# A two-layer encoder on one core: idle TensorE products and a pinned order at the opening, earlier q swaps and later value products in the last layer

## The chip, the core and the metric

The kernel runs on one core of a Trainium2 chip. A core has five engines that work side by side, each in the order of its own instruction stream: TensorE (PE in the profile, with its weight loads shown as PEld), VectorE (DVE), ScalarE (ACT), GpSimd (POOL) and SyncE (SP), which here only issues transfers (DMAs). They wait for each other through semaphores. The metric is the time of one execution in microseconds; less is better.

## The reference

Two layers over 272 tokens (16 learned ones and 256 given) of width 2048. Cut to what matters:

```python
for i in range(DEPTH):                                  # DEPTH = 2
    h = _rmsnorm(h_stream, norm_mix[i])
    proj = h @ w_in[i]                                  # q | k | v | f | ga | gf
    q = _rope_2d(_rmsnorm(q, q_norm[i]), cos_r, sin_r, cos_c, sin_c)     # 8 heads of 128
    k = _rope_2d(_rmsnorm(k, k_norm[i]), cos_r, sin_r, cos_c, sin_c)     # 2 heads
    s = einsum('bqkgd,bskd->bkgqs', q, k) / sqrt(128);  p = softmax(s);  attn = einsum(p, v)
    a_br = attn @ w_attn_br[i]
    s_br = fft2(f over tokens and group channels).real @ w_four[i]
    merged = sigmoid(ga) * a_br + sigmoid(gf) * s_br
    h_stream = h_stream + merged @ w_out[i]
    h2 = _rmsnorm(h_stream, norm_ffn[i])
    u_gate = _dwconv3_centred((h2 @ w_up[i])[..., :D_FF], w_conv[i], b_conv[i])
    h_stream = h_stream + (silu(u_gate) * (h2 @ w_up[i])[..., D_FF:]) @ w_down[i]
return h_stream[:, N_META:]
```

All is float32.

## The kernel before

**Tiling.** Activations lie channels by tokens: 16 tiles of 128 channels x 272 tokens. To keep float32 accuracy each operand is split into a high part and the remainder (`xH`, `xL`; `wh`, `wl`), and each product is made of three: high x high, high x low, low x high. Weights stream in chunks of 512 KB (four blocks of 128 rows x 256 columns). One chunk is loaded into one of four `raw` buffers by SP (`load_raw`, L264), ACT casts it into `wh` (L306), DVE subtracts that into `wl` (L308), and TensorE multiplies it: 24 products of 272 columns.

**Order.** A planner orders each engine's instructions by the order in which they are traced and by when it thinks that their inputs are there. `tc.keep_in_program_order` pins an instruction behind the one traced before it on its engine. `tc.manual_schedule` keeps the traced order of the engines that it names for a whole block.

**Groups and shadow work.** `group` runs the products of one block of weight columns. After every six products it calls `step`, which advances one of the generators in `shadow` (work that shares the engines with the groups: norms, rotary embedding, Fourier transform, attention). A `yield n` asks for n steps of pause; `push(gen, n)` starts a generator after n steps. `next_split` calls `advance`, which loads ahead by the four buffers, and `pump`, which traces the casts and subtractions.

**The opening.** Four columns of the layer's Fourier projection come first (`first_groups`, L420 on), two at a time, while XT and the first weights still arrive. Chunk 0 comes in pieces (L486 to L488) and so do the first tiles of XT; `norm_split` (L520) makes `xH` on ACT and `xL` on DVE, and `norm_sum` (L527) squares a tile on ACT and adds it up on DVE for the norm. The load of chunk 1 (L491) waits for a tiny GpSimd copy into its buffer (L490), which itself reads chunk 0.

**The last layer's mixing part.** The order of groups is k, v, q0, q1, f4 (the folded Fourier columns, `folded_f`), q2, q3, then the gates ga and gf. For each q group `head_evac` (L927) leaves the scaled heads in `qp` and their squares in `qps`; `q_stage` (L1037) swaps 32-row blocks with four transfers on SP (`swap`, L946), sums the squares through TensorE transposes, and rotates (`rope`, L952). `kstats` (L975) does the same for k. `attend` runs `attention` once for each of the two k heads: per item scores (L1085), softmax (`normalise`), transposes of the weights into `PH` and `PL` (`transposed`, L1116), and per head the value products (`values`, L1138), whose operands are `PH` and `PL` of the whole head. The items follow each other step by step in the loop at L1148.

Of the kernel before, what the change touches and what calls it, by code (L numbers as in the profile page):

```python
# [10 lines left out]
F32 = mybir.dt.float32  # L11
# [150 lines left out]
def encoder_kernel(ctx, tc, xT, params, consts, bmat, cfold, csign, w_fl, w_f64c, w_in, w_abr, w_four, w_f64, w_out, w_up, w_down, w_vn, w_dn, w_dt, out):  # L162
# [79 lines left out]
            chunks.append(ch)  # L242
    st = {"raw": 0, "fetch": 0, "next": 0, "grp": 0, "stage": None}
    raws, splits = {}, {}
    RAW, LOOK = 4, 2

    def extra(i):
# [51 lines left out]
    def split_w(i, a, b, parts="hl"):  # L299
        if i not in splits:  # L300
            splits[i] = tuple(weight_rows(wp.tile([P, CW * CS], F32R, tag=t, name=f"{t}{i}"), i in streamed) for t in ("wh", "wl"))
        h, lo = splits[i]
        st["wl"] = lo
        r = raws[i]
        if "h" in parts:
            nc.scalar.copy(h[:, a:b], r[:, a:b])  # L306
        if "l" in parts:
            nc.vector.tensor_tensor(lo[:, a:b], r[:, a:b], h[:, a:b].bitcast(F32), op=ALU.subtract)  # L308
            if b == CW:
                del raws[i]  # L310

# [165 lines left out]
    o64m = per.tile([P, P], F32, name="o64m")  # L477
    small = ctx.enter_context(tc.tile_pool(name="small", bufs=4))

    nc.gpsimd.dma_start(remE[:, 0, 0:1], chunks[1][0][:, 0, 0:1])  # L480
    nc.gpsimd.memset(mhalf, -0.5)
    nc.scalar.dma_start(prm[:, 0:P_BG], params[:, 0:P_BG])
    nc.scalar.activation(warm, mhalf[:, 0:1], AF.Copy)
    r0 = wp.tile([P, CW, MG * P], F32, tag="raw", name="raw0", bufs=RAW)
# [2 lines left out]
        nc.sync.dma_start(XT[:, c0:c1, :], xT[:, c0:c1, :])  # L487
        nc.sync.dma_start(r0[:, c0:c1], chunks[0][0][:, c0:c1])  # L488
    raws[1] = wp.tile([P, CW, MG * P], F32, tag="raw", name="raw1", bufs=RAW)
    nc.gpsimd.tensor_copy(raws[1][:, 0, 0:1], r0[:, 0, 0:1])  # L490
    tc.keep_in_program_order(nc.sync.dma_start(raws[1], chunks[1][0]))  # L491
    tc.keep_in_program_order(nc.sync.dma_start(XT[:, 4:8, :], xT[:, 4:8, :]))
    load_raw(2)
    load_raw(3)
    st["raw"] = 4
    tc.keep_in_program_order(nc.sync.dma_start(XT[:, 8:12, :], xT[:, 8:12, :]))
    nc.gpsimd.memset(ones, 1.0)
    nc.gpsimd.memset(V3.bitcast(F32), 0.0)
    nc.gpsimd.memset(o64.bitcast(F32), 0.0)
    nc.gpsimd.memset(o64m, 0.0)  # L500
    nc.gpsimd.memset(remE, 0.0)
# [18 lines left out]
    def norm_split(m, goff):  # L520
        gc = prm[:, goff + m:goff + m + 1]
        xH, xL = (xHLs[goff // KT % DEPTH][:, r] for r in range(2))
        nc.scalar.activation(xH[:, m, :], XT[:, m, :], AF.Copy, scale=gc)
        nc.vector.scalar_tensor_tensor(xL[:, m, :], XT[:, m, :], gc, xH[:, m, :].bitcast(F32),
                                       op0=ALU.mult, op1=ALU.subtract)

    def norm_sum(m):  # L527
        sq = small.tile([P, T], F32, tag="sq", name="sq", bufs=2)
        nc.scalar.activation(sq, XT[:, m, :], AF.Square)
        if m == 0:  # L530
            nc.vector.tensor_copy(acc, sq)
        else:
            nc.vector.tensor_tensor(acc, acc, sq, op=ALU.add)
# [100 lines left out]
    for l in range(DEPTH):  # L634
# [7 lines left out]
        with tc.tile_pool(name=f"mix{l}", bufs=1) as mp:  # L642
# [105 lines left out]
            if l == 0:  # L748
                def sums(pss):
                    for m in range(KT):  # L750
                        norm_sum(m)
                        yield 4 if m % 4 == 3 else 1
                    yield from norm_stats(hold, 4)
                    yield 3
                    for i in range(2):
                        f_evac(i, pss[i])
                        yield 2
                    hold["evac"] = True

                pss = []  # L760
                push(sums(pss), 4)
                first_groups(pss)
                for dst, src in ((cst[:, 0:C_MASK], consts[:, 0:C_MASK]), (cst[:, C_CC:], consts[:, C_CC:]), (prm[:, P_BG:], params[:, P_BG:])):
                    tc.keep_in_program_order(nc.sync.dma_start(dst, src))
                bt = rt("bt")
                bt = bt[:, :, :TH]
                tc.keep_in_program_order(nc.sync.dma_start(bt, bmat.rearrange("p (a b) -> p a b", a=2)))
                with tc.manual_schedule(engines={mybir.EngineType.PE, mybir.EngineType.DVE}):
                    ps = group((l, "f", 2), xr(0), T, "aux")
                until(hold, "evac")  # L770
                f_evac(2, ps)
                nc.scalar.copy(BH, bt)
                tc.keep_in_program_order(nc.vector.tensor_tensor(BL, bt, BH.bitcast(F32), op=ALU.subtract))
                nc.gpsimd.memset(br3[96:P].bitcast(F32), 0.0)
                for a in (0, 32):
                    nc.scalar.copy(br3[a:a + 32], brem[a:a + 32])
                tc.keep_in_program_order(nc.vector.tensor_tensor(br3[64:96], brem[32:64], br3[32:64].bitcast(F32), op=ALU.subtract))
                tc.keep_in_program_order(nc.vector.tensor_scalar(bgh, prm[:, P_BG:P_BG + DEPTH * 2 * KT], 0.5, None, op0=ALU.mult))
                f_evac(3, group((l, "f", 3), xr(0), T))
            else:  # L780
                push(norm_stats(hold), 8)
                nc.gpsimd.memset(remE, 0.0)
                nc.gpsimd.memset(remO, 0.0)
                w64c = rw("w64c").rearrange("p a b -> p (a b)")[:, :KT * NG].rearrange("p (k r) -> p k r", k=KT)
                nc.sync.dma_start(w64c, w_f64c)
                w64s = mp.tile([P, 2, 2 * TH], F32R, tag="r", name="w64s", bufs=7)
                w64s = w64s.rearrange("p a b -> p (a b)")[:, :KT * 2 * NG].rearrange("p (k r) -> p k r", k=KT)
                nc.scalar.copy(w64s[:, :, 0:NG], w64c)
                nc.vector.tensor_tensor(w64s[:, :, NG:], w64c, w64s[:, :, 0:NG].bitcast(F32), op=ALU.subtract)
# [185 lines left out]
            def kstats():  # L975
# [4 lines left out]
                nc.vector.tensor_scalar(kss, kss, 1.0 / HD, EPS, op0=ALU.mult, op1=ALU.add)  # L980
                rk = small.tile([P, 2, 3], F32, tag="rk", name="rk")
                pow_half(rk.rearrange("p a b -> p (a b)"), kss.rearrange("p a b -> p (a b)"))
                yield 6
                for kv in range(NKV):
                    dk = ut("dk")
                    for i, (a, b) in enumerate(BLK):
# [8 lines left out]
                yield from rope(kp, qs, kH, kL)  # L995
                hold["keys"] = True

            push(kstats(), 4)
            if last:
                slots = fold_setup()  # L1000
                push(fold_ahead(slots), 2)
# [32 lines left out]
            for pn in pns:  # L1034
                nc.gpsimd.memset(pn[:, 0:P], 0.0)

            def q_stage(i, qp, qsq):  # L1037
                kv, j = i // 2, i % 2
                sl = slice(2 * j, 2 * j + 2)
                if j == 0:  # L1040
                    qvs.append(small.tile([P, 9], F32, tag="qv", name="qv"))
                    qsms.append(small.tile([P, 2, 4, NM], F32, tag="sqm", name="sqm", bufs=2))
                qv, qsm = qvs[kv], qsms[kv]
                qs = swap(qp)
                yield 3
                nc.vector.tensor_copy(qsm[:, :, 2 * j:2 * j + 2, :], qsq[:, :, 0:NM].unsqueeze(1).to_broadcast([P, 2, 2, NM]))
                d4 = qv[:, 4 * j:4 * j + 4]
                sums_t(d4, [qsq[:, m, a:b] for m in range(MG) for a, b in BLK[1:]])
                d4 = d4.rearrange("p (m i) -> p m i", m=2)
                nc.vector.tensor_tensor(d4, d4, bc2(tok2[:, 1:3]), op=ALU.mult)  # L1050
                if j:
                    yield 1
                    sums_t(qv[:, 8:9], [qsm.rearrange("p r h t -> p (r h t)")])
                    nc.vector.tensor_tensor(qv[:, 8:9], qv[:, 8:9], tok2[:, 0:1], op=ALU.mult)
                    nc.vector.tensor_scalar(qv, qv, 1.0 / HD, EPS, op0=ALU.mult, op1=ALU.add)
                    rq = small.tile([P, 9], F32, tag="rq", name="rq")
                    pow_half(rq, qv)
                yield 6 - j
                yield from rope(qp, qs, qH[kv][:, sl, :], qL[kv][:, sl, :])
                if j:  # L1060
                    rqs.append(rq)
                    if kv == 0:
                        push(attend(), 5)
# [7 lines left out]
                    yield from attention(kv, rqs[kv])  # L1071

            def attention(kv, rq):
                nc.vector.tensor_scalar(rq, rq, 1.0 / math.sqrt(HD), None, op0=ALU.mult)
                qm = mp.tile([P, 2, 2, 4, NM], F32R, tag="qm", name="qm")
                for j, src in enumerate((qH, qL)):
                    nc.scalar.copy(qm[:, j], src[kv][:, :, 0:NM].bitcast(F32).unsqueeze(1).to_broadcast([P, 2, 4, NM]))
# [68 lines left out]
                    nc.vector.tensor_tensor(qL[kv][:, h, lo:T], po[:, :W], qH[kv][:, h, lo:T].bitcast(F32), op=ALU.subtract)  # L1146

                items = [None] + [(h, i) for h in range(4) for i in range(2)]  # L1148
                prev, ready, due = None, [], []
                for item in items + ["end", "end"]:  # L1150
                    cur = None
                    if item != "end":
                        pe, sm = scores(item)
                    yield 2
                    if item != "end":
                        cur = (item, normalise(pe, sm))
                    yield 1
                    if prev is not None:
# [1 line left out]
                        if prev[0] is not None and prev[0][1] == 1:  # L1160
                            due.append(prev[0][0])
                        yield 1
                    if ready:
                        values(ready.pop(0))
                    if prev is not None:
                        yield 1
                    ready, due = ready + due, []
                    prev = cur
                while ready:
                    values(ready.pop(0))  # L1170
                    yield 1

            qH, qL = [], []
            for i in range(4):
# [17 lines left out]
                if last and i == 1:  # L1192
# [5 lines left out]
                            folded_f(slots, E)  # L1198
                    o1_tiles()
                    push(folded_chan(E), 1)  # L1200
                push(q_stage(i, *qq), 1)


            def gate(kind, i):
# [401 lines left out]
```

## Time and profile before

| what | time |
|---|---|
| median of 3 runs | 2517.09 us (2516.09 to 2518.9) |
| profiled execution, its own time | 2520.21 us |
| its span, first to last instruction | 2518.4 us |
| mean granted TensorE clock over the span | 0.998 |
| TensorE busy | 2503.5 us |

The span is what the views of the trace show; the execution's own time is 1.8 us longer. In lists of waits the columns are: who waited, for whom, then the total in us, how often, and the longest. In a timeline: start, length in us, engine, line, operation, what it writes and reads, and in brackets the engine's idle time before it with what ended that. Merged rows have a count (x4).

### The profile page before, as it was taken

The numbers are of one execution on the slowest core, as the hardware profiler recorded it, in microseconds if no ns is written. First come the engines' busy times: TensorE is split into PE (matmuls) and PEld (weight loads), VectorE is DVE, ScalarE is ACT, GpSimd is POOL, SyncE is SP. The second block draws the span as 40 slices with busy tenths as digits, with TensorE's granted clock in tenths as the row PEclk, the third lists the DMA queues.
The fourth block names the chain that finished last, engine by engine and source line by source line (L and its number), as shares of the span: only waits on it lengthen the run. The fifth ranks groups of instructions, "written<-read, shape, count | busy, mean of one in ns | idle before, by whom it ended". The sixth has DMA issues, their size and how long they took to land. (4 is left out here: it accounts for less than half of the span.)

```text
span 2518.4 us, 47932 instructions
## 1 busy us (share of the span) xinstructions
PE 2503.5 (99%) x18848; PEld 2423.2 (96%) x18848; DVE 1988.6 (79%) x3159; ACT 1339.9 (53%) x1913; POOL 203.9 (8%) x394
## 2 busy tenths in 40 slices
PE   9999999999999999999999999999999999999999
PEld 9999999999999999999999999999988899999987
DVE  7687866778878677888768877666879787898898
ACT  6455534454444334444445555444676665666665
POOL 0000000012212222222200000000000000000000
PEclk9999999999999999999999999999999999999999
DMA  7444557879999999999975547888888887788887
GB/s 248 166 156 163 188 198 245 261 267 378 396 335 378 407 384 374 397 381 379 400 268 177 193 141 224 272 262 261 259 260 293 298 289 241 260 282 290 280 301 272
DMA packets 194802, 706.85 MB, mean 281 GB/s; under 512 B 22144, under 2 KB 27392, under 8 KB 194320
## 3 DMA queue, kind: packets, MB, share of 16 engines
q1 hardware_dynamic: 146768, 517.09, 58.4%
q0 software_dynamic: 46368, 184.57, 21.1%
q8 instruction: 147, 2.41, 0.4%
q10 hardware_dynamic: 1440, 2.13, 0.2%
q14 instruction: 79, 0.65, 0.1%
HBM read 623.32 MB, written 111.15 MB: 292 GB/s over the span
## 5 line engine op out<-in xcount | busy, mean ns | idle before, releaser
L306 ACT CAST wh<-raw 128x1024 fp32r<-128x1024 f32 (+1 forms) x961 | 998.6, 1044 | 888.9 <-PE ps_ug L378 190.2
L308 DVE TENSOR_TENSOR wl<-raw,wh 128x1024 fp32r<-128x1024 f32 (+1 forms) x961 | 1159.2, 1218 | 391.0 <-ACT wh L306 378.1
L377 PE MATMUL ps_ug<-xHL,wh 128*128 128x272 f32 (+1 forms) x1408 | 401.1, 285 | 0.0
L379 PE MATMUL ps_ug<-xHL,wl 128*128 128x272 f32 (+1 forms) x1408 | 399.4, 285 | 0.0
L378 PE MATMUL ps_ug<-xHL,wh 128*128 128x272 f32 (+1 forms) x1408 | 399.1, 284 | 0.0
L377 PEld LDWEIGHTS ps_ug<-xHL,wh 128*128 128x128 f32 x1408 | 265.4, 188 | 3.2
L378 PEld LDWEIGHTS ps_ug<-xHL,wh 128*128 128x128 f32 x1408 | 265.0, 188 | 3.2
L379 PEld LDWEIGHTS ps_ug<-xHL,wl 128*128 128x128 f32 x1408 | 264.7, 188 | 1.1 <-DVE wl L308 0.4
L1446 PE MATMUL ps_p<-wh,opnd 128*128 128x512 f32 x816 | 222.3, 393 | 0.0
L379 PE MATMUL ps_uv<-xHL,wl 128*128 128x272 f32 x704 | 202.2, 287 | 0.0
L379 PE MATMUL ps_d<-gHL,wl 128*128 128x272 f32 x704 | 202.1, 287 | 0.0
L377 PE MATMUL ps_uv<-xHL,wh 128*128 128x272 f32 x704 | 201.7, 286 | 0.0
L377 PE MATMUL ps_d<-gHL,wh 128*128 128x272 f32 x704 | 201.5, 286 | 0.0
L378 PE MATMUL ps_uv<-xHL,wh 128*128 128x272 f32 x704 | 201.0, 285 | 0.0
L378 PE MATMUL ps_d<-gHL,wh 128*128 128x272 f32 x704 | 201.0, 285 | 0.0
L1446 PEld LDWEIGHTS ps_p<-wh,opnd 128*128 128x128 f32 x816 | 148.5, 188 | 28.5 <-ACT wh L306 0.2
L377 PE MATMUL ps_ga<-xHL,wh 128*128 128x272 f32 (+1 forms) x512 | 148.6, 290 | 0.0
L377 PE MATMUL ps_gf<-xHL,wh 128*128 128x272 f32 (+1 forms) x512 | 147.0, 287 | 0.0
L540 DVE TENSOR_TENSOR wi<-wi,wi 128x512 f32<-128x512 f32 x224 | 146.9, 685 | 0.0
L378 PE MATMUL ps_ga<-xHL,wh 128*128 128x272 f32 (+1 forms) x512 | 146.2, 286 | 0.0
L379 PE MATMUL ps_ga<-xHL,wl 128*128 128x272 f32 (+1 forms) x512 | 146.2, 286 | 0.0
L379 PE MATMUL ps_o<-mH,wl 128*128 128x272 f32 (+1 forms) x512 | 146.0, 285 | 0.0
(380 smaller groups left out, 5974.0 us busy)
## 6 DMA issues: line engine op xcount, KB each, us to landing
raw<-in_w_up SPq DMA_DIRECT2D x288, 512.0 KB, 6.4
raw<-in_w_in SPq DMA_DIRECT2D x191, 512.0 KB, 4.2
raw<-in_w_down SPq DMA_DIRECT2D x88, 512.0 KB, 7.3
wi<-in_w_dn POOLq DMA_DIRECT2D x80, 512.0 KB, 9.3
ft<-wi POOLq DMA_DIRECT2D x80, 512.0 KB, 7.7
raw<-ft SPq DMA_DIRECT2D x80, 512.0 KB, 4.7
raw<-in_w_out SPq DMA_DIRECT2D x64, 512.0 KB, 4.2
raw<-fv SPq DMA_DIRECT2D x64, 512.0 KB, 4.8
```

Source lines behind the costliest of these rows:

```text
L306: nc.scalar.copy(h[:, a:b], r[:, a:b])
L308: nc.vector.tensor_tensor(lo[:, a:b], r[:, a:b], h[:, a:b].bitcast(F32), op=ALU.subtract)
L377: nc.tensor.matmul(o, h[:, c, sl], a, start=kt == 0, stop=False)
L378: nc.tensor.matmul(o, h[:, c, sl], b, start=False, stop=False)
L379: nc.tensor.matmul(o, lo[:, c, sl], a, start=False, stop=kt == nk - 1)
L540: tt = lambda *v, **kw: tc.keep_in_program_order(nc.vector.tensor_tensor(*v, **kw))
L1446: nc.tensor.matmul(ps[h], x, w[:, 512 * h:512 * h + 512], start=fresh and (s_, q) in BEGIN and first, stop=(s_, q) in END and end, skip_gr ...
```

## The change

At the opening: `V3` is zeroed by DVE first instead of by GpSimd later, and 14 products of the zeroed `V3` with itself (128 x 128 by 128 x 256) go to TensorE into a PSUM tile that nobody reads. The GpSimd copy ahead of chunk 1's load is gone and that load is made of two halves. The splits of chunk 0, of the first four tiles of XT, and the first four squares are pinned in traced order.

In the last layer: the k statistics start two steps later and pause two steps less before the next part; the four swap transfers of each q pair are traced right behind `head_evac`, that is before the next group's loads, instead of in the first step of `q_stage`; and a head's value products are held until the next item's scores have been traced, two steps later than before.

In both layers: the q statistic keeps its sum and adds EPS * HD instead of being divided by HD, so that the power of -1/2 holds the factor 1/sqrt(HD), and the scaling of `rq` in `attention` is gone.

```diff
@@ split_w
+        keep = in_order if i == 0 else lambda v: v
         if "h" in parts:
-            nc.scalar.copy(h[:, a:b], r[:, a:b])
+            keep(nc.scalar.copy(h[:, a:b], r[:, a:b]))
...
@@ opening
+    nc.vector.memset(V3.bitcast(F32), 0.0)
     nc.gpsimd.dma_start(remE[:, 0, 0:1], chunks[1][0][:, 0, 0:1])
     nc.gpsimd.memset(mhalf, -0.5)
+    idle = psum.tile([P, 512], F32, tag="aux", name="ps_idle")
+    for _ in range(14):
+        nc.tensor.matmul(idle[:, :NKV * P], V3[:, 0, :], V3.rearrange("p a b -> p (a b)"), start=True, stop=True)
...
-    nc.gpsimd.tensor_copy(raws[1][:, 0, 0:1], r0[:, 0, 0:1])
-    tc.keep_in_program_order(nc.sync.dma_start(raws[1], chunks[1][0]))
+    for c0 in (0, 2):
+        in_order(nc.sync.dma_start(raws[1][:, c0:c0 + 2], chunks[1][0][:, c0:c0 + 2]))
...
-    nc.gpsimd.memset(V3.bitcast(F32), 0.0)
...
@@ norm_split, norm_sum
+        keep = in_order if goff == P_NM and m < CW else lambda v: v
...
+        keep = in_order if opening and m < CW else lambda v: v
         sq = small.tile([P, T], F32, tag="sq", name="sq", bufs=2)
-        nc.scalar.activation(sq, XT[:, m, :], AF.Square)
+        keep(nc.scalar.activation(sq, XT[:, m, :], AF.Square))
...
@@ kstats
-                yield 6
+                yield 4 if last else 6
...
-            push(kstats(), 4)
+            push(kstats(), 6 if last else 4)
...
@@ q_stage, attention
-                qs = swap(qp)
+                if qs is None:
+                    qs = swap(qp)
...
-                    nc.vector.tensor_scalar(qv, qv, 1.0 / HD, EPS, op0=ALU.mult, op1=ALU.add)
+                    nc.vector.tensor_scalar(qv, qv, EPS * HD, None, op0=ALU.add)
...
-                nc.vector.tensor_scalar(rq, rq, 1.0 / math.sqrt(HD), None, op0=ALU.mult)
...
-                    yield 2
+                    if held:
+                        yield 1
+                        values(held.pop(0))
+                        yield 1
+                    else:
+                        yield 2
...
-                    if ready:
+                    if ready and not last:
                         values(ready.pop(0))
                     if prev is not None:
                         yield 1
-                    ready, due = ready + due, []
+                    if last:
+                        held, ready, due = held + ready, due, []
+                    else:
+                        ready, due = ready + due, []
                     prev = cur
+                ready = held + ready
...
-                push(q_stage(i, *qq), 1)
+                push(q_stage(i, *qq, swap(qq[0]) if last else None), 1)
```

More of the change, by code (lines that the diff above doesn't have):

```diff
@@ L244, in encoder_kernel @@
     raws, splits = {}, {}
+    in_order = tc.keep_in_program_order
     RAW, LOOK = 4, 2
@@ L304, in split_w @@
         r = raws[i]
+        keep = in_order if i == 0 else lambda v: v
         if "h" in parts:
-            nc.scalar.copy(h[:, a:b], r[:, a:b])
+            keep(nc.scalar.copy(h[:, a:b], r[:, a:b]))
         if "l" in parts:
-            nc.vector.tensor_tensor(lo[:, a:b], r[:, a:b], h[:, a:b].bitcast(F32), op=ALU.subtract)
+            keep(nc.vector.tensor_tensor(lo[:, a:b], r[:, a:b], h[:, a:b].bitcast(F32), op=ALU.subtract))
             if b == CW:
@@ L522, in norm_split, with norm_sum @@
         xH, xL = (xHLs[goff // KT % DEPTH][:, r] for r in range(2))
[L523 to L527, printed above, removed]
+        keep = in_order if goff == P_NM and m < CW else lambda v: v
+        keep(nc.scalar.activation(xH[:, m, :], XT[:, m, :], AF.Copy, scale=gc))
+        keep(nc.vector.scalar_tensor_tensor(xL[:, m, :], XT[:, m, :], gc, xH[:, m, :].bitcast(F32),
+                                            op0=ALU.mult, op1=ALU.subtract))
+    def norm_sum(m, opening=False):
+        keep = in_order if opening and m < CW else lambda v: v
         sq = small.tile([P, T], F32, tag="sq", name="sq", bufs=2)
-        nc.scalar.activation(sq, XT[:, m, :], AF.Square)
+        keep(nc.scalar.activation(sq, XT[:, m, :], AF.Square))
         if m == 0:
@@ L750, in sums @@
                     for m in range(KT):
-                        norm_sum(m)
+                        norm_sum(m, True)
                         yield 4 if m % 4 == 3 else 1
@@ L1035, in encoder_kernel, with q_stage @@
                 nc.gpsimd.memset(pn[:, 0:P], 0.0)
-            def q_stage(i, qp, qsq):
+            def q_stage(i, qp, qsq, qs=None):
                 kv, j = i // 2, i % 2
@@ L1148, in attention @@
                 items = [None] + [(h, i) for h in range(4) for i in range(2)]
-                prev, ready, due = None, [], []
+                prev, held, ready, due = None, [], [], []
                 for item in items + ["end", "end"]:
```

## The prediction

> **What bounds the kernel now.** I read the page's busy table first, then the list of TensorE's waits over the whole span, then busy time and granted clock by stretch around each wait, and last the order of time on the engine that is waited for.
>
> ```profile
> PE 2503.5 (99%) x18848; PEld 2423.2 (96%) x18848; DVE 1988.6 (79%) x3159; ACT 1339.9 (53%) x1913; POOL 203.9 (8%) x394
> ...
> PE ps_f L444 <- ACT wh L306: 4.8, 2, 4.5
> PE ps_pv L1142 <- DVE PL L1134: 2.9, 3, 1.8
> PE ps_f L873 <- DVE wl L308: 2.7, 1, 2.7
> PE ps_ss L943 <- DVE sqm L972: 0.4, 1, 0.4
> ```
>
> TensorE is the bound. It is idle for 2518.4 - 2503.5 = 14.9 us, and four rows name 10.8 of them. The change touches all four places; no other edit could be worth much. Beyond the idle time, TensorE runs slowly after some waits:
>
> ```profile
> 4.50:11.25 6.75, 6.42 (x26) 6.10 (x27) 4.81 (x12) 4.38 (x11) 0.33 (x2) 1.00 0.89 327
> 11.25:20.35 9.10, 9.10 (x74) 9.10 (x74) 8.94 (x19) 9.10 (x20) 0.00 (x0) 1.00 1.03 408
> ...
> 1366.70:1369.41 2.71, 0.00 (x0) 0.00 (x0) 2.05 (x5) 0.65 (x1) 0.00 (x0) 1.00 0.01 3
> 1369.80:1376.60 6.80, 6.80 (x34) 6.63 (x34) 5.32 (x8) 3.28 (x6) 0.00 (x0) 0.51 0.67 232
> 1376.60:1403.70 27.10, 27.10 (x235) 26.73 (x234) 23.06 (x33) 18.59 (x28) 0.24 (x2) 1.00 0.79 252
> ...
> 1459.00:1460.85 1.85, 0.06 (x2) 0.01 (x1) 1.85 (x6) 1.68 (x4) 0.00 (x0) 1.00 0.82 283
> 1461.95:1465.30 3.35, 3.35 (x18) 3.35 (x18) 2.32 (x7) 0.75 (x3) 0.00 (x0) 0.52 0.45 159
> 1465.40:1500.00 34.60, 34.50 (x287) 34.09 (x286) 24.48 (x59) 18.32 (x36) 0.00 (x0) 1.00 0.42 147
> ```
>
> The columns are length, busy time of PE, its loads, DVE, ACT and POOL, granted clock, DMA share and GB/s. After the idle 2.71 us the clock is 0.51 for 6.80 us: 6.80 x 0.49 = 3.3 us lost. After the 1.85 us it is 0.52 for 3.35 us: 1.6 us lost. In the opening the clock column says 1.00, yet 26 products take 6.42 us (0.247 each) against 74 in 9.10 (0.123): 26 x 0.124 = 3.2 us lost there too. So the change can reach 0.4 + 2.7 + 3.3 + 3.1 (below) + 1.6 in the last layer, 11.1 us, and 3.2 us plus some waiting in the opening.
>
> **The k statistics.** They start two steps later, and two steps less follow, so all behind them stays in place. A step is six products, 6 x 34.60 / 287 = 0.72 us; two make 1.4 us, more than the 0.4 us that the transposes wait for the copy of the squares. Gain 0.4 (bounds 0 and 0.4).
>
> **The q swap ahead of the loads.** What holds `wl` back for 2.72 us is ahead of it on DVE:
>
> ```profile
> 1358.03 0.32 SPq L264 DMA_DIRECT2D raw<-fw  x1
> 1358.45 2.56 SPq L949 DMA_DIRECT2D qs<-qp  x4
> ...
> raw<-fw SPq DMA_DIRECT2D x7, 512.0 KB, 3.3
> ...
> qs<-qp SPq DMA_DIRECT2D x4, 68.0 KB, 3.1
> ...
> 1355.72 0.48 DVE L936 SCALAR_TENSOR_TENSOR qp<-ps_q,prm,rstdB 128x258 f32<-128x258 f32 x1
> ...
> 1359.42 2.36 DVE L308 TENSOR_TENSOR wl<-raw,wh 128x1024 fp32r<-128x1024 f32 x2
> 1364.62 0.73 DVE L953 TENSOR_TENSOR qs<-qs,cst 128x544 f32<-128x544 f32 x1 [2.84 <-DMA qs<-qp]
> ...
> 1367.50 0.73 DVE L958 TENSOR_TENSOR q<-qp,q 128x544 fp32r<-128x544 f32 x1 [0.66 <-ACT q L956]
> 1368.14 1.22 DVE L308 TENSOR_TENSOR wl<-raw,wh 128x1024 fp32r<-128x1024 f32 x1
> ...
> 1426.04 0.73 DVE L953 TENSOR_TENSOR qs<-qs,cst 128x544 f32<-128x544 f32 x1
> ...
> 1364.60 1.04 ACT L306 CAST wh<-raw 128x1024 fp32r<-128x1024 f32 x1
> ...
> 1369.41 0.93 PE L873 MATMUL ps_f<-hA,wl 128*128 128x138 f32 x5 [2.72 <-DVE wl L308]
> ```
>
> Head pair 0 is ready at 1355.72 + 0.48 = 1356.20, but its four swaps go out at 1358.45, behind a weight load that waited for a buffer. DVE works in order, so its 2.84 us for the swapped copy delay `wl`, and TensorE with it. With the swap traced before the next group's loads, it can go out at 1356.2; four take 2.56 us, the last is issued near 1358.2 and lands 3.1 us later (the median), 1361.3. Before, the last of the four took about 4.2 us (issued near 1360.4, used at 1364.62); by that it is 1362.4. DVE is free at 1359.42 + 2.36 = 1361.78. So the stall of 2.84 becomes 0 to 0.6, `wl` ends at 1366.5 to 1367.2 instead of 1369.36, and TensorE, out of work at 1366.70, waits 0 to 0.5. I take 0.3, because the transfer's median is nearer: 2.4 us gained. The two slow stretches follow the two longest waits (2.72 and 1.8); a wait of 0.3 should leave none, so the 3.3 us of half clock go too.
>
> What is late next: the stage to 1403.70 starts about 5.7 us earlier and DVE must keep up. It is busy 23.06 of 27.10 us there, 4.0 us to spare, but in lumps (a folded sum every third chunk); I give back 0.5 (0 to 3). The load behind the swap goes out near 1358.8 instead of 1358.03, 0.8 later; it would have landed at 1358.03 + 3.3 = 1361.3 for the cast at 1364.60, so 2.5 us remain. Swaps 2 and 3 can push a load by up to the 2.56 that four issues take; I take 0, since TensorE's list has no wait for a transfer (price otherwise in rival 4). Swap 1 is traced behind the f4 stage, pinned behind a load of its end; its copy is read only at 1426.04. Together 2.4 + 3.3 - 0.5 = 5.2 (bounds 0 and 6.0).
>
> **Value products two steps later, and one scale less.** At the first value product:
>
> ```profile
> 1449.72 0.17 DVE L1074 TENSOR_SCALAR rq<-rq 128x9 f32<-128x9 f32 x1 [1.91 <-POOL rq L518]
> ...
> 1460.39 0.41 DVE L1134 TENSOR_TENSOR PL<-ps_pt,PH 128x256 fp32r<-128x256 f32 x1
> ...
> 1456.16 0.49 PE L1120 MATMUL ps_pt<-cst,pn 128*128 128x128 f32 x3
> ...
> 1460.85 0.39 PE L1142 MATMUL ps_pv<-PL,VH 128*128 128x258 f32 x1 [1.79 <-DVE PL L1134]
> ...
> L1142 PE MATMUL ps_pv<-PL,VH 128*128 128x258 f32 x16 | 5.1, 322 | 3.1 <-DVE PL L1134 2.9
> ```
>
> DVE finishes the low part of the transposed weights 4.6 us after its transposes, and the value product stands one step behind them. The removed scaling of `rq` (L1074) cost DVE 1.91 us of waiting for GpSimd shortly before; folding the scale into EPS * HD removes that wait (the scores that need `rq` of the second half come much later). Two steps give another 1.4 us. 1.91 + 1.4 covers the 1.79; the other two waits are 2.9 - 1.8 = 1.1 together, each under 1.4. So all 3.1 go, and the 1.6 us of half clock behind the long one. Work is only moved: the sweep has as many steps, and the last head's product stays where it was. A held product now stands between scores and transposes and keeps its PSUM tile there; I give back 0.3. Gain 4.4 (bounds 0 and 4.7).
>
> **The opening.**
>
> ```profile
> 1.19 1.28 ACT L483 ACT_TABLE_LOAD   x1 [1.19 <-PEq L1598]
> 3.74 0.41 ACT L529 ACTIVATE sq<-XT 128x272 f32<-128x272 f32 x1
> 4.05 0.39 ACT L306 CAST wh<-raw 128x256 fp32r<-128x256 f32 x1
> 5.37 0.52 ACT L523 ACTIVATE xHL<-XT,prm 128x272 fp32r<-128x272 f32 x1 [0.92 <-DMA XT<-in_xT]
> 9.71 1.14 ACT L306 CAST wh<-raw 128x512 fp32r<-128x512 f32 x2 [1.20 <-DMA raw<-in_w_in]
> ...
> 3.07 0.43 SPq L488 DMA_DIRECT2D raw<-in_w_in  x1
> 5.42 0.33 SPq L491 DMA_DIRECT2D raw<-in_w_in  x1
> ...
> 4.28 0.36 DVE L531 COPY acc<-sq 128x272 f32<-128x272 f32 x1
> 19.12 1.23 DVE L308 TENSOR_TENSOR wl<-raw,wh 128x1024 fp32r<-128x1024 f32 x1
> ...
> 20.51 0.29 PE L446 MATMUL ps_f<-xHL,wl 128*128 128x272 f32 x1
> ```
>
> The first square stands ahead of the first cast; fixing the order takes its 0.31 us (4.05 - 3.74) from the start. The 14 idle products of 256 columns take 14 x 0.247 x 256/272 = 3.3 us. They need the zeroed V3. DVE shows no memset; a copy of like size takes 0.36, and ACT's first work starts at 1.19, so the products start near 1.6 and end near 4.9, or up to half a microsecond sooner, where the first cast would let real work begin near 4.05 - 0.31 + 0.39 = 4.1, and did at 4.5. They may cost 0.5. In return the clock is up sooner, at most 3.2 us. But data pace the opening: ACT waits for transfers at 5.37 and 9.71, and the fifth `wl` ends at 19.12 + 1.23 = 20.35, just when TensorE wants it (20.51). The second chunk's load is freed of its GpSimd copy and can leave when SP has issued the first (3.07 + 0.43), 1.9 us before 5.42, into DMA engines that are 89% busy; and four squares with their adds move into the stretch where ACT is busy 9.10 of 9.10 us. A faster TensorE would mostly wait there, and a wait of 1.85 us was enough to lose the clock. I take 0.7 (bounds -0.5 and 3.8), nearer to the data's side.
>
> **Sum.** 0.4 + 5.2 + 4.4 + 0.7 = 10.7 us. The profiled execution took 2520.21 us (its span and 1.8 around it), so 2509.5 by its own time. It lies 3.1 above the median of the runs, 2517.09; some runs probably pay less for slow stretches than this one did. Taken from the median the sum gives 2506.4; I take the middle, 2508.
>
> **Rivals**, with the changes counted from 2508. (1) The idle products' warmth survives: for it speak the 26 slow products, against it the clock lost after 1.85 us. Then the opening gives 3.2 + 0.3 = 3.5 instead of 0.7: 2505. [...] (2) One last-layer site stays, most likely because DVE's order shifts and the value product meets a new wait: without the 4.4, 2512.4. (3) The waits only move: DVE, 79% busy, meets another late input at both sites, and 0.4 + 0.7 are left of the sum: 2517.09 - 1.1 = 2516. For it: DVE's order is planned with assumed times. Against it: the late inputs have names and each edit removes one. (4) Slower: the swaps at the head of SP's queue hold the weight loads until `qp` exists. It decides where the wait for `qp` uses up the 2.5 us that the loads have left; each of three swaps then costs 2.6 us and a half-clock stretch of 3.3: 17.6, less the 6.0 already paid at the first, less the 5.5 gained elsewhere, + 6.1: 2523. Against it: `qp` was ready 2.25 us before its swap left.
>
> **Numbers.** Forecast 0.50, (1) 0.10, (2) 0.15, (3) 0.15, (4) 0.10. 0.2% is 5.0 us, about what a measurement of this kernel can tell from no change; so under 2512.1 is faster: 0.50 + 0.10 + half of (2) = 0.68; same 0.07 + 0.15 = 0.22; slower 0.10. Range 2504 to 2517: from (1) with a little more at the sites to (3), leaving out (4) and the tails.
>
> **What would show it.** No DVE wait for qs<-qp near 1360, the L873 wait under 0.5 and a clock near 1.00 through the f4 stage; no L1074 and under 0.5 of L1142 waits; no ps_ss wait; 14 products before the first real one, and the time at which product spacing halves from about 0.25 us. The forecast is wrong if f4 shows new waits for `wl` over 3 us, if ACT's casts there wait for raw<-fw, or if the idle products end after 4.9.

## The result, and the profile after

| | before | after |
|---|---|---|
| median of 15 runs, us | 2516.9 (2514.45 to 2522.0) | 2512.98 (2511.16 to 2514.87) |
| ratio to before, 95% interval | | 0.9981 [0.9974, 0.9988] |
| profiled execution, its span, us | 2520.21, 2518.4 | 2511.16, 2509.4 |

Faster by 3.9 us between the medians, or by 4.8 (3.0 to 6.5) by the ratio, where 9.1 were forecast. The two profiled executions differ by 9.05 us, for a reason that the runs below show: the one of before was among the slowest of its kind, the one of after the fastest.

The busy table's first line and the list of TensorE's waits (in all, times, longest, in us) of the changed kernel:

```profile
PE 2499.5 (100%) x18862; PEld 2418.7 (96%) x18862; DVE 1987.9 (79%) x3156; ACT 1340.8 (53%) x1913; POOL 204.0 (8%) x392
...
PE ps_f L880 <- DVE wl L310: 2.2, 1, 2.2
PE ps_f L446 <- ACT wh L308: 1.6, 3, 1.0
...
PE ps_pv L1149 <- DVE PL L1141: 0.6, 1, 0.6
PE ps_kb L997 <- DVE dk L994: 0.4, 1, 0.4
```

TensorE's idle time fell from 14.9 to 2509.4 - 2499.5 = 9.9 us. But 3.1 us of that fall are the 14 idle products, which count as busy while TensorE would still have waited for its first weights (they start at 1.20, the first real product at 4.35):

```profile
1.20 3.35 PE L487 MATMUL ps_idle<-V 128*128 128x256 f32 x14 [1.20 <-DVE V L482]
```

So only some 1.9 us of waiting went, since the opening's waits behind the first product grew from 0.3 to 1.6. The value products' waits went from 2.9 to 0.6. But f4 still waits 2.2 us for `wl`, where 0 to 0.5 was forecast, and the 0.4 us that the k statistics waited at the transposes (`ps_ss`) is now waited one step on, at `ps_kb` for `dk`: fewer steps are left for the power on GpSimd and the scaling.

What holds `wl` in f4, in the order of time of DVE (start, length, then what ended the idle time before it):

```profile
1354.45 0.49 DVE L943 SCALAR_TENSOR_TENSOR qp<-ps_q,prm,rstdB 128x258 f32<-128x258 f32 x1
...
1356.12 1.22 DVE L310 TENSOR_TENSOR wl<-raw,wh 128x1024 fp32r<-128x1024 f32 x1
1357.26 0.72 DVE L962 TENSOR_TENSOR kp<-kp,qs 128x544 f32<-128x544 f32 x1
1357.89 0.48 DVE L943 SCALAR_TENSOR_TENSOR qp<-ps_q,prm,rstdB 128x258 f32<-128x258 f32 x1
...
1363.47 0.72 DVE L960 TENSOR_TENSOR qs<-qs,cst 128x544 f32<-128x544 f32 x1 [1.29 <-DMA qs<-qp]
...
1367.00 1.22 DVE L310 TENSOR_TENSOR wl<-raw,wh 128x1024 fp32r<-128x1024 f32 x1
```

and of SP's queue:

```profile
1357.37 0.33 SPq L265 DMA_DIRECT2D raw<-fw  x1
1358.53 3.32 SPq L956 DMA_DIRECT2D qs<-qp  x4
```

The swap is ahead in the program, yet it leaves at 1358.53; before it left at 1358.45. The copy of the second half of head pair 0 now starts 3.44 us after that of the first half, because a `wl` and an addition for the keys were put between them; before, it ended at 1356.20. The swap waits for it. And one more weight load, 1357.37, still goes ahead.

Two stretches of the first stage (length, busy time and count of PE, its loads, DVE, ACT, POOL, clock, DMA share, GB/s), of before:

```profile
4.50:13.35 8.85, 8.52 (x43) 8.20 (x44) 6.86 (x16) 6.48 (x16) 0.33 (x2) 1.00 0.92 340
13.35:28.90 15.55, 15.55 (x128) 15.55 (x127) 15.43 (x29) 13.87 (x29) 0.00 (x0) 1.00 0.84 307
```

and the same of after, with what follows the wait in f4:

```profile
4.50:13.35 8.85, 7.25 (x49) 6.36 (x48) 5.63 (x13) 5.83 (x13) 0.20 (x1) 1.00 0.96 355
13.35:28.90 15.55, 15.55 (x121) 15.20 (x122) 15.45 (x29) 14.29 (x30) 0.00 (x0) 1.00 0.78 290
...
1368.30:1376.60 8.30, 8.27 (x69) 7.98 (x70) 7.10 (x12) 4.63 (x7) 0.00 (x0) 1.00 0.64 201
```

With the idle products TensorE is six products ahead at 13.35 us, 49 against 43; at 28.90 it has lost them, 121 against 128. DVE is busy 15.45 of the 15.55 us: the splits pace the stage. In f4 the clock stayed at 1.00 after the wait of 2.2 us, where before it fell to 0.51.

### The profile page after: what moved, and what is told of

Read it like the earlier page. It is cut to its first block, busy times and chain, and to the rows that moved or that the text cites. A ratio compares the mean times of both kernels' runs of the same rounds, so it can differ in the third digit from the quotient of the medians.

```text
span 2509.4 us, 47962 instructions
## 1 busy us (share of the span) xinstructions
PE 2499.5 (100%) x18862; PEld 2418.7 (96%) x18862; DVE 1987.9 (79%) x3156; ACT 1340.8 (53%) x1913; POOL 204.0 (8%) x392
## 4 chain that ended last, share of the span: by engine, by line
PE 97%; DVE 1%; DMA 1%; issue 0%; ACT 0%; SPq 0%; POOL 0%; DVEq 0%; ACTq 0%
PE ps_p L1462 14%; PE ps_ug L381 7%; PE ps_ug L379 7%; PE ps_ug L380 7%; PE ps_d L381 3%; PE ps_uv L381 3%; PE ps_uv L379 3%; PE ps_d L379 3%; PE ps_uv L380 3%; PE ps_d L380 3%; PE ps_ga L379 2%; PE ps_o L381 2%; PE ps_ga L380 2%; PE ps_o L379 2%; PE ps_ga L381 2%; PE ps_gf L379 2%
## 5 line engine op out<-in xcount | busy, mean ns | idle before, releaser
L379 PE MATMUL ps_o<-mH,wh 128*128 128x272 f32 (+1 forms) x512 | 145.5, 284 | 0.0
```

The source lines that it names most:

```text
L379: nc.tensor.matmul(o, h[:, c, sl], a, start=kt == 0, stop=False)
```

## The experiments

All runs were timed against the kernel before, which had medians of 2516.8 to 2517.6 us. Times are medians with the range of the runs; the waits are those of the profiled execution. Gains are given as differences of medians, or, where an interval stands beside them, as the ratio times 2517 us; the two can differ by about 1 us.

| run | us | ratio, 95% interval | f4 wait | value waits |
|---|---|---|---|---|
| 1 no k statistics' shift | 2510.37 (2509.58 to 2511.14) | 0.9972 [0.9960, 0.9983] | 0.3 | 0.6 |
| 2 swap alone | 2513.23 (2512.17 to 2515.16) | 0.9983 [0.9974, 0.9991] | 0.3 | 2.5 |
| 3 values alone | 2511.54 (2509.32 to 2514.80) | 0.9976 [0.9966, 0.9986] | 1.4 | 0.6 |
| 4 opening alone | 2515.88 (2514.65 to 2520.00) | 0.9995 [0.9986, 1.0004] | 1.7 | 2.5 |
| 5 no idle products | 2510.21 (2508.93 to 2510.87) | 0.9974 [0.9965, 0.9984] | 0.4 | 0.6 |
| 6 held values alone | 2512.67 (2511.11 to 2520.96) | 0.9985 [0.9977, 0.9993] | 1.4 | 1.7 |
| 7 swap and values | 2509.26 (2508.76 to 2510.90) | 0.9973 [0.9963, 0.9983] | 0.4 | 0.6 |
| 8 and a late rotation | 2508.98 (2508.51 to 2509.72) | 0.9969 [0.9958, 0.9980] | none | 0.6 |
| 9 filled f4 wait | 2511.99 (2511.30 to 2512.58) | 0.9980 [0.9971, 0.9989] | filled | 0.6 |
| 10 bridged opening | 2510.49 (2509.76 to 2511.39) | 0.9976 [0.9966, 0.9986] | 1.0 | 0.6 |
| 11 swap with k statistics | 2517.25 (2512.91 to 2521.71) | 0.9996 [0.9987, 1.0005] | 1.0 | 2.7 |

**1. Without the k statistics' shift.** The theory from the traces: the shift, not the swap edit, moved DVE's order.

```diff
-                yield 4 if last else 6
+                yield 6
-            push(kstats(), 6 if last else 4)
+            push(kstats(), 4)
```

> The changed kernel with the k statistics put back where they were before. Theory A (the k statistics moved DVE's order: the copy of the second half of head pair 0 went behind a wl, to 1357.89, and the swap with it): here that copy runs near 1355.7 again, the four swaps go out near 1356.3 instead of 1358.53 and land near 1361.5 instead of 1363.35, DVE waits under 0.5 us for them instead of 1.29, and TensorE waits 1.0 us or less for wl in the f4 stage instead of 2.2. The wait of 0.4 us at ps_kb goes and one of 0.4 at ps_ss is back. Time 2510 to 2512, against 2513.0 for the changed kernel. Rival B (the swap's own transfer sets the wait, wherever it leaves): TensorE still waits 2 us or more in f4, and the time is 2513, no different.

DVE, and then SP's queue, in the same stretch of this run, whose profiled execution is 1355.25 - 1354.45 = 0.8 us later here:

```profile
1355.25 0.48 DVE L943 SCALAR_TENSOR_TENSOR qp<-ps_q,prm,rstdB 128x258 f32<-128x258 f32 x1
...
1356.92 0.48 DVE L943 SCALAR_TENSOR_TENSOR qp<-ps_q,prm,rstdB 128x258 f32<-128x258 f32 x1
...
1362.89 0.72 DVE L960 TENSOR_TENSOR qs<-qs,cst 128x544 f32<-128x544 f32 x1
```

```profile
1357.54 2.52 SPq L956 DMA_DIRECT2D qs<-qp  x4
```

and its waits (the first belongs to the opening):

```profile
PE ps_f L446 <- ACT wh L308: 1.9, 2, 1.2
...
PE ps_f L880 <- DVE wl L310: 0.3, 1, 0.3
```

The copies are 1.67 us apart again, the swap leaves 2.29 us after the first copy instead of 4.08, DVE does not wait for it, and f4 waits 0.3 us. Theory A holds: taking out an edit that was to gain 0.4 us made the kernel 2.6 us faster by the medians, and the two ranges do not meet (the intervals of the ratios overlap). Rival B is out: f4 does not wait 2 us whenever the swap leaves.

**2, 3, 4. Each part alone** in the kernel before: the swap; the held value products with the scale in the constant; the opening. Their diffs are those of the change.

> The kernel before with nothing but the q swap ahead of the weight loads (last layer). Theory A (the swap's gain is there once nothing holds its copy back): swaps leave near 1356.3, the f4 wait is 1.0 us or less instead of 2.7 and leaves no half clock behind it; 1.7 us of wait and 0 to 3.3 us of half clock go: 2512 to 2515, against 2516.9 before. Rival B (the swap's own transfer sets the wait): 2516.5 to 2517, f4 wait over 2 us.

> The kernel before with only the value products two steps later and the scale of rq folded into the constant. Theory A: the three waits of the value products (2.9 us by the list, 4.1 from start to start) fall to under 1, and the half clock of up to 1.7 us behind the longest goes in the runs that had it: 2512 to 2513.8, against 2516.9 before. Rival C (the value products meet another late input, the waits only move): 2516 to 2517 with waits of 2 us or more elsewhere between 1445 and 1545 us.

> The kernel before with only the opening's edits (idle products, fixed order, split load). Theory D (transfers and the splits pace the opening, TensorE's lead of 0.7 us at the second chunk is given back by the end of the first stage): the product at 31.9 us comes 0.0 to 0.1 us sooner, time 2516.5 to 2517, no different from before. Rival E (the forecast's 0.7 us stays): that product comes 0.5 to 0.8 us sooner, time near 2516.2.

Waits of the swap alone, and of the values alone:

```profile
PE ps_pv L1143 <- DVE PL L1135: 2.5, 3, 1.7
PE ps_f L873 <- DVE wl L308: 0.3, 1, 0.3
```

```profile
PE ps_f L873 <- DVE wl L308: 1.4, 1, 1.4
PE ps_pv L1141 <- DVE PL L1133: 0.6, 1, 0.6
```

The swap alone gives the forecast's wait of 0.3 us exactly, and 2517 x 0.0017 = 4.3 us (2.3 to 6.5 by the interval); Rival B is out again. The values alone give 6.0 us (3.5 to 8.6), a little more than expected; Rival C is out. The opening alone can't be told from nothing (1.3 us faster, between 3.5 faster and 1.0 slower).

Runs 3 and 4 do not touch the swap, and yet f4 waits 1.4 and 1.7 us in them, not 2.7. DVE's row for the swapped copy, in run 4:

```profile
1364.80 0.73 DVE L960 TENSOR_TENSOR qs<-qs,cst 128x544 f32<-128x544 f32 x1 [1.83 <-DMA qs<-qp]
```

From the first of its four issues to this first use the swap took 6.2 us before, 5.2 in run 4, 4.4 in run 3, 4.9 in the changed kernel, 4.2 in run 11 and 5.8 in run 10, where it left early and f4 still waited 1.0 us. So the wait in one profiled execution depends on when the swap leaves and also on how long it takes; what sets the second is open.

The opening's trace agreed with neither guess. The first product of the second group stands at 31.89 us before, 31.84 after, and in run 4 at 32.51:

```profile
31.89 0.29 PE L377 MATMUL ps_f<-xHL,wh 128*128 128x272 f32 x1
```

```profile
32.51 0.29 PE L379 MATMUL ps_f<-xHL,wh 128*128 128x272 f32 x1
```

It came 0.6 us later than before, in an execution whose clock fell during the stage, which no theory had named; run 10 tests that. The waits of the opening alone, and its windows (the clock is the third number from the end):

```profile
PE ps_pv L1149 <- DVE PL L1141: 2.5, 3, 1.7
PE ps_f L446 <- ACT wh L308: 2.1, 2, 1.5
PE ps_f L880 <- DVE wl L310: 1.7, 1, 1.7
```

```profile
4.85:8.25 3.40, 1.85 (x11) 1.36 (x10) 1.09 (x3) 1.50 (x4) 0.00 (x0) 1.00 0.90 268
8.76:11.60 2.84, 2.84 (x12) 2.84 (x13) 2.38 (x4) 1.50 (x3) 0.00 (x0) 0.50 1.01 397
...
1370.20:1373.50 3.30, 3.30 (x17) 3.22 (x17) 1.95 (x3) 1.75 (x2) 0.00 (x0) 0.50 0.70 189
...
1459.40:1470.00 10.60, 10.60 (x87) 10.40 (x88) 8.92 (x23) 5.81 (x13) 0.00 (x0) 1.00 0.48 153
```

The values alone, after f4's wait:

```profile
1366.96:1368.80 1.84, 1.83 (x16) 1.84 (x16) 1.84 (x3) 0.33 (x1) 0.00 (x0) 1.00 0.45 102
1368.90:1372.25 3.35, 3.35 (x18) 3.27 (x17) 2.66 (x5) 1.77 (x3) 0.00 (x0) 0.50 0.81 256
```

In one and the same execution of run 4 the clock was at half behind the opening's wait of 1.5 us (to 11.60) and f4's of 1.7 us (to 1373.50), and stayed up behind the value product's wait of 1.7 us (from 1459.40). In run 3 it fell 1.9 us after a wait of 1.4; in the changed kernel it held after 2.2. So of these waits of 1.4 to 2.2 us some were followed by half clock and some were not, and what one profiled execution pays for them does not stand for all.

**5. Without the 14 idle products** (on run 1's kernel).

```diff
-    for _ in range(14):
-        nc.tensor.matmul(idle[:, :NKV * P], V3[:, 0, :], ...)
```

> The changed kernel with the k statistics back (as in the run without their shift, 2510.4) and without the 14 idle products; the fixed order and the split load stay. Theory D (transfers and splits pace the first stage; the warmth that the idle products give is lost again in its waits of 0.5 to 1.5 us): the product at 28.9 us before comes between 28.4 and 29.7, as with them, and the time is 2510 to 2511. Rival E (the idle products carry a gain of their own): that product 0.5 us or more later than with them (over 30.1), time 2511 or more. Rival H (they cost time: the clock that they bring up falls at the next wait): time 2509.0 to 2509.8.

2510.21 against 2510.37, with ranges that overlap: Theory D as to the time; the idle products gain and cost nothing that can be told. The second group begins at 32.10 us, no later than in run 1 (32.59). Rivals E and H have no support in this; an effect well under 1 us, either way, would not show.

**6. Held value products alone**, the scaling of `rq` kept.

> The kernel before with only the value products two steps later; the scaling of rq stays. Theory A1 (the two steps alone cover the long wait): the waits of the value products fall to 0.6 to 1 us in all and the time is 2511 to 2513, like the run with both. Rival (the forecast's: the 1.79 us wait needs the 1.91 us of the scaling and the two steps): a wait of 0.3 to 1 us stays at the first value product and another 0.6 later, 2513 to 2514.

Its profiled execution took 2520.96 us, slower already before the last layer: from 500 to 1200 us it got through 5593 products where run 3 got through 5654, both at a granted clock of 1.00. Why is open. Only its waits, and one stretch behind them, are read:

```profile
PE ps_pv L1142 <- DVE PL L1134: 1.7, 2, 1.1
PE ps_f L873 <- DVE wl L308: 1.4, 1, 1.4
```

The first value product still waits 1.1 us, 0.1 more than the rival's upper end, and another 0.6 stays: the forecast's reading, that the scaling's 1.91 us and the two steps are both needed, holds by the trace. The median of 2512.67, against 2511.54 with both, lies in Theory A1's range; the times of whole executions don't decide here, the intervals overlap. The stretch from the last q product to the last ga product, which holds the value products, does by the traces: 309.4 us without both edits (runs 2, 4 and 11, clock up), 307.2 with the two steps alone, 305.9 with both (run 3).

**7 and 8. Towards a version that beats both.** Only swap and values, with opening and k statistics as before; then head pair 0's rotation four steps later, so that f4's second `wl` goes ahead of it on DVE.

```diff
-                yield 6 - j
+                yield 6 - j + (4 if last and i == 0 else 0)
```

> The kernel before with the q swap ahead of the loads and the value products later with the folded scale; opening and k statistics as before. If the two sites are independent and the opening and the k statistics give nothing: f4 wait 0.35 us, value waits 0.6, no half clock after 1330 us, and the time equals or beats that of the changed kernel without the k statistics' shift: 2508.5 to 2510.5. If the opening's edits do carry 0.7 us, 2511 or more.

> As the one before, and head pair 0's rotation four steps later in the last layer, so that the wl which f4 needs second goes ahead of it on DVE. If DVE's work of 3.5 us for the rotation is what is left of the f4 wait: that wait goes from 0.35 to 0, and the time falls by 0.3 to 0.5, to 2508 to 2510. Rival: the rotation then holds the next wl, needed near 1368.7, and a wait of 0.5 to 1.5 us appears one chunk later: 2509 to 2512.

Both came out as first expected. In run 8's list of waits no `wl` is left in f4, and what is behind it waits 0.2 us:

```profile
PE ps_f L869 <- DVE qp L936: 0.2, 1, 0.2
```

Run 8 is the fastest kernel here: 2508.98 us, and its slowest run (2509.72) is below the changed kernel's fastest (2511.16). It uses half of the change and one more line. Between 7 and 8 the times don't tell. Neither was timed beside the changed kernel, only beside the kernel before.

**9. The f4 wait filled.** In the changed kernel, 30 products of 128 columns into columns that nobody reads, ahead of the wait.

```diff
+                    if k == 1:
+                        h, lo_, sl = wx[0]
+                        for _ in range(30):
+                            nc.tensor.matmul(ps[0][1][:, 2 * TH:3 * TH], h[:, 0, 0:P], sl[:, 0, 0, :], start=False, stop=False)
```

> The changed kernel with 30 products of 128 columns, into unused columns of a PSUM tile, between f4's first chunk and the wait for the second chunk's wl. They leave that wait's end where it is and only keep TensorE at work through most of it. Theory F (a wait of 1.4 to 2.7 us there drops the clock to half in some executions and not in others, and this is why the changed kernel's median of 2513.0 lies 1.8 us above its profiled 2511.2): no stretch at 0.5 between 1360 and 1380 us, the wl still ends near 1368.2, and the median falls to 2511 to 2512.3. Rival G (the spread comes from elsewhere, the opening above all): median 2512.7 to 2513.3, as without them.

Windows of the wait and of what follows:

```profile
1365.80:1368.30 2.50, 2.50 (x24) 2.50 (x24) 1.77 (x2) 1.87 (x3) 0.00 (x0) 1.00 0.28 115
1368.40:1376.00 7.60, 7.57 (x66) 7.25 (x66) 6.22 (x11) 3.65 (x6) 0.00 (x0) 1.00 0.67 205
```

The useful work begins again at 1368.4, close to the changed kernel's 1368.28, but TensorE was never idle. The median falls by 1.0 us (the ratios, 0.9980 and 0.9981, do not show it) and the range from 3.7 us (2511.16 to 2514.87) to 1.3 us. The granted clocks decide for Theory F: over the whole execution the mean was under 1.000 in 14 of the changed kernel's 15 executions, all but the one that was profiled, and in 1 of 11 here. So half clock at this wait is what most executions of the changed kernel pay and its profile does not show.

The same count fits the other kernels. Of 75 executions of the kernel before, the 14 with a mean clock of 1.000 have a median of 2514.2 us, the 40 with 0.999 one of 2517.0, the 21 with 0.998 one of 2519.6. It was 1.000 in all executions of runs 2, 7 and 8. By an estimate from these traces a stretch of 3.35 us at half clock lowers the mean by 3.35 x 0.5 / 2510 = 0.0007, so it would show. That run 2 is among them says that half clock behind the value products' wait, which run 2 keeps, came in none of its 11 executions.

**10. The opening bridged** (run 1's kernel): 14 more idle products in its waits.

```diff
+            for _ in range({1: 2, 2: 8, 4: 4}.get(kt, 0)):
+                nc.tensor.matmul(idle[:, :NKV * P], V3[:, 0, :], ...)
             for m in range(MG):
```

> The kernel of the run without the k statistics' shift (2510.4), with 2, 8 and 4 further idle products ahead of the second, third and fifth kt of the opening, to keep TensorE at work in its waits there. Theory I (the opening's edits lose 0.7 us in executions in which the clock falls again at a wait of 1 to 1.5 us near 7 to 8.7 us): no stretch at 0.5 before 29 us after the clock has come up, the product at 28.9 us before comes at 28.4 to 29.0 instead of 29.6, and the median falls to 2509.3 to 2510. Rival D (splits and transfers pace the stage whatever the clock does): that product stays at 29.0 to 29.7 and the median at 2510 to 2511.

A window of the stage, then the first product of the second group, here and in run 1:

```profile
12.00:29.10 17.10, 17.10 (x134) 16.55 (x133) 16.99 (x33) 15.87 (x34) 0.00 (x0) 1.00 0.80 293
```

```profile
32.06 0.29 PE L379 MATMUL ps_f<-xHL,wh 128*128 128x272 f32 x1
```

```profile
32.59 0.29 PE L379 MATMUL ps_f<-xHL,wh 128*128 128x272 f32 x1
```

The clock holds, and the second group begins 0.5 us sooner than in run 1's profiled execution, whose clock fell, as Theory I had it; but no sooner than before (31.89), with DVE busy 16.99 of 17.10 us. The time is 2510.49 against 2510.37: Rival D. The clock of the opening is worth nothing that the median shows; DVE's share says that the splits set the stage's end.

**11. Swap with the k statistics' shift**, no opening edits.

> The kernel before with the q swap ahead of the loads (which alone gave 2513.2) and the k statistics' shift, nothing else. Theory A (the shift alone moves DVE's order and takes the swap's gain): the copy of the second half runs near 1357.9, swaps leave near 1358.5, f4 waits 1.5 to 2.5 us, 2514.5 to 2516.5. Rival B (the shift does it only with the opening's edits): swaps leave near 1356.3, f4 waits under 0.6, 2513.

DVE's order in it:

```profile
1353.42 0.49 DVE L936 SCALAR_TENSOR_TENSOR qp<-ps_q,prm,rstdB 128x258 f32<-128x258 f32 x1
...
1355.09 1.22 DVE L308 TENSOR_TENSOR wl<-raw,wh 128x1024 fp32r<-128x1024 f32 x1
...
1356.86 0.48 DVE L936 SCALAR_TENSOR_TENSOR qp<-ps_q,prm,rstdB 128x258 f32<-128x258 f32 x1
```

The copies are 3.44 us apart, as in the changed kernel: the shift does it without the opening's edits, so Rival B is out. The f4 wait was 1.0, less than expected, and the median 2517.25, 0.7 above what Theory A expected and 4.0 above the swap alone. That this shift costs the swap's gain is shown by the medians (the intervals of the two ratios just overlap). The granted clock points at half clock as the way: it was 1.000 in three executions, of which two took 2512.91 and 2512.94, as quick as the swap alone; in the eight under 1.000, none of which was profiled, the times are 2513.97 to 2518.28. The third at 1.000 is the slowest of all, 2521.71; its cause is open, as in run 6's profiled execution.

## Why the prediction was right in kind and too large

**The step that failed** is the k statistics': "They start two steps later, and two steps less follow, so all behind them stays in place." What is traced behind them stays; but DVE's order is planned, and the shift changed it a group of products further on (runs 1 and 11). The next sentence to fall was "Head pair 0 is ready at 1355.72 + 0.48 = 1356.20": it was ready at 1357.89 + 0.48 = 1358.37, and the swap, freed of the loads, waited for it. So of the 2.4 us for the stall only 2.72 - 2.22 = 0.5 came in the changed kernel's profiled execution, and what was left of the wait was long enough for half clock in the others (run 9). This one miss is 2.6 of the 5.0 us between forecast and result (run 1: 2510.37).

**The other 2.4 us** (2508 to 2510.37) come from the starting point and the opening more than from the two large terms. Two stretches of the last layer, in each profiled execution, from the start of one product to the start of another, in us:

| | before | changed | run 1 | run 2 | run 3 | run 4 | run 6 | run 7 |
|---|---|---|---|---|---|---|---|---|
| f4's first product to the last of q3 | 72.6 | 69.1 | 67.7 | 67.3 | 69.7 | 70.0 | 68.4 | 67.3 |
| from there to the last of ga | 311.3 | 305.9 | 306.0 | 309.4 | 305.9 | 309.4 | 307.2 | 305.9 |

- *The swap's 5.2 us.* Against the profiled execution of before it was right to 0.1: 72.6 - 67.3 = 5.3 in runs 2 and 7. But 3.3 of this are half clock. Run 6, which has neither the swap edit nor half clock, takes 68.4, so the order alone is worth about 1.1 there. By the times of run 2 the edit is worth 4.3 (2.3 to 6.5).
- *The value products' 4.4 us.* Right in mechanism (both edits needed, run 6) and a little small: 311.3 - 305.9 = 5.4 against the same execution, of which the list of waits names only 2.9 - 0.6 = 2.3 and half clock is 1.6 to 1.9. With the clock up the edit is worth 309.4 - 305.9 = 3.5. The times of run 3 give 6.0 (3.5 to 8.6), which does not exclude 4.4. The 0.6 of wait that is left is at the later sweep, at 1523 us.
- *The starting point.* The terms were read from one execution with half clock at both sites, so they belong to its 2520.21: the sum from there gave 2509.5, and runs 1, 5 and 7 have medians of 2510.4, 2510.2 and 2509.3. Subtracted from the median, they also take off half clock that the median execution did not pay. The prediction saw this ("some runs probably pay less") and took the middle, which is 1.5 us too low. For the same reason the two parts give 4.3 and 6.0 us alone and 6.8 together (run 7; 4.3 to 9.3); that this is less than their sum is likely, but the intervals overlap.
- *The opening's 0.7 us.* The reason was right, data pace it; but then the answer is 0, not 0.7. The second chunk's load left at 3.56 instead of 5.42, and its cast still waited for it:

```profile
3.56 0.91 SPq L497 DMA_DIRECT2D raw<-in_w_in  x2
...
9.64 0.62 ACT L308 CAST wh<-raw 128x512 fp32r<-128x512 f32 x1 [0.77 <-DMA raw<-in_w_in]
```

Before, that cast ran at 9.71. The idle products cost no start: the memset on DVE took 0.27 us from 0.87, so they start at 1.20, where the estimate had about 1.6, and the first real product came at 4.35 instead of 4.50.

**The rivals.** (1) fell: in the changed kernel's profile the clock did hold through the opening, and the lead was lost to the splits all the same; in two others (runs 1 and 4) it fell at the waits of 1.2 and 1.5 us. (2) came nearest in time, 2512.4, but at the other site: it was f4 that stayed, not the value products. (3) was true of the k statistics alone. (4) did not appear: no wait for a transfer is in TensorE's list. The signs asked for were met at the opening's 14 products and at `ps_ss`, missed by 0.1 us at the value products (0.6, where under 0.5 was asked), and missed at f4: DVE waited 1.29 us for the swap, TensorE 2.2 for `wl`. The clock near 1.00 through f4 was met by luck, with the wait still there.

## What to carry to other kernels

Where a planner orders an engine's work, an edit that moves steps in one place can reorder another; read the order of the instructions that the other edits rely on (here two copies of one tile) before adding terms up. A gain read from one profiled execution that contains half clock belongs to that execution: take it from that execution's own time, or price the wait in full and the clock behind it in part, and look at how the times and granted clocks of the other executions spread. Two edits that each pass alone are worth testing together and each without the other: here half of the change, with one line more, beat the whole.

## What was not expected of the hardware

Windows behind the opening's wait of 1.2 us in run 1 (which follows another of 0.8 within 3.1 us), behind the value product's 1.7 in run 2, and behind the 1.4 and 1.1 us of run 6:

```profile
8.62:11.50 2.88, 2.88 (x12) 2.88 (x13) 2.35 (x4) 2.01 (x5) 0.00 (x0) 0.50 1.01 401
```

```profile
1454.70:1470.00 15.30, 15.28 (x127) 15.08 (x128) 12.69 (x33) 8.02 (x18) 0.00 (x0) 1.00 0.47 145
```

```profile
1377.30:1390.00 12.70, 12.68 (x108) 12.29 (x109) 11.86 (x18) 7.80 (x12) 0.00 (x0) 1.00 0.74 237
1465.70:1480.00 14.30, 14.29 (x120) 14.30 (x121) 12.16 (x31) 7.67 (x18) 0.00 (x0) 1.00 0.46 149
```

So the clock fell after waits of 2.7 and 1.8 us (before), 1.7 and 1.4 (runs 4 and 3), and 1.5 and 1.2 in the opening (runs 4 and 1); it held after 2.2 (after), 1.8 and 1.0 (run 11), 1.7 (runs 2 and 4), 1.4 and 1.1 (run 6). In these traces the length of a wait between 1.2 and 2.2 us did not decide by itself. The stretches at half clock in the last layer: 3.35 us at 0.52 and 6.80 at 0.51 before, 3.30 and 3.35 at 0.50 in runs 4 and 3, each with a clock of 1.00 right behind it. Why one wait is followed by half clock and another of the same length is not stays open; no run here tests it. A wait of 1.4 us in run 3, with no other near it, was followed by it.

That half clock came late: TensorE worked 1.9 us at a clock of 1.00 after run 3's wait before the clock fell.
